# A row sum over 16,384 rows: one row a partition loaded first, and a tail of 15 rows a partition

## The chip, the core and the metric

The kernel runs on one core of one Trainium2 chip. The metric is the time on the device in microseconds (us), the median of several runs. The engines used are VectorE (DVE in the profile), ScalarE (ACT) and SyncE (SP), whose queue issues every DMA. TensorE does nothing here and GpSimd (POOL) only sets four constants. The 16 DMA engines of the core move the data between the chip's memory (HBM) and the on-chip memory, which has 128 partitions.

## The reference

```python
def setup_inputs():
    batch, seq, dim = 32, 512, 1024
    return {
        "x": np.random.randn(batch, seq, dim).astype(np.float32),
        "multiplier": 0.5,
    }

def reference(x, multiplier):
    return (np.sum(x, axis=-1) * multiplier).astype(np.float32)
```

x has 32 x 512 = 16,384 rows of 1024 float32 numbers (4 KB a row, 67.1 MB in all). Each row becomes one number: its sum times 0.5. The output is 64 KB.

## The kernel before

Each of the 128 partitions handles 128 rows. The rows lie in two regions of x. The first region, `x_rows`, gives each partition 112 consecutive rows (`own`), so that neighbouring partitions' rows lie 112 x 4 KB = 448 KB apart. The second, `x_last`, gives each partition 16 consecutive rows, 64 KB apart from partition to partition.

The first region is worked off in seven blocks of 16 rows a partition (line 105). A block is one load of 8.4 MB into one of three buffers `xb`; in it each partition has one stretch of 64 KB. VectorE sums the block in one instruction into `sums` (line 117) and scales the sums into `res` (line 123). A load into a buffer waits until VectorE has summed what lay there (line 77, by the counts in `freed`). In the seventh block VectorE sums eight rows, and ScalarE the other eight, one `activation` with an accumulator each (line 82).

The second region is the tail (lines 137 to 172). It goes into the next buffer in three pieces, rows 0 to 7, 8 to 12, and 13 to 14; row 15 goes into a tile of its own, `end`, in two parts of 608 and 416 columns. Each part has a semaphore. The set `on_act` says which rows ScalarE takes; VectorE takes the others with `dve_sum` (line 92), which adds the halves of a row and accumulates. The two parts of row 15 are summed by VectorE, `first` and `final`, where the second takes up the sum of the first through one column of `end`.

All DMAs stand on SP's queue in program order: seven blocks, three pieces, two parts of the last row, then the store of the first region's results (`early`, line 150, 448 bytes a partition), then the store of the tail's results (line 175, 64 bytes a partition). `early` waits for the seventh block's sums on both engines, the last store for the `final` sum and for ScalarE's last row. At the end SP waits for both stores.

`start_loads_at_entry` (line 182) moves the loads at the head of SP's queue that wait for nothing, up to the first one that waits, from the body of the program to its entry, ahead of the barrier at which all engines meet. These are the first three blocks' loads.

Of the kernel before, what the change touches and what calls it, by code (L numbers as in the profile page):

```python
# [8 lines left out]
@with_exitstack  # L9
def kernel(  # L10
    ctx: ExitStack,
    tc: tile.TileContext,
    x: bass.AP,
    multiplier: float,
    out: bass.AP,
):

    nc = tc.nc
    tc.close()
    tc.compile()  # L26
    nc.switch_body("work")

    P = nc.NUM_PARTITIONS
    fp32 = mybir.dt.float32  # L30
    ADD = mybir.AluOpType.add

    x_flat = x.flatten_outer_dims()
    N, D = x_flat.shape
    rows = N // P
    out_flat = out.rearrange("b s -> (b s)")
    mul = float(multiplier)

    B = 16
    n_blocks = rows // B  # L40
    assert N == P * rows and rows == n_blocks * B
    own = rows - B
    x_rows = x_flat[0 : P * own, :].rearrange("(p c) d -> p c d", p=P)
    x_last = x_flat[P * own : N, :].rearrange("(p c) d -> p c d", p=P)
    out_rows = out_flat[0 : P * own].rearrange("(p c) -> p c", p=P)
    out_last = out_flat[P * own : N].rearrange("(p c) -> p c", p=P)

    def sbuf(name, *shape):
        return ctx.enter_context(nc.sbuf_tensor(name, list(shape), fp32)).ap()

    bufs = 3
    buf = [sbuf(f"xb{i}", P, B, D) for i in range(bufs)]
    sums = sbuf("sums", P, rows)
    res = sbuf("res", P, rows)
    cut = 608
    at = 640
    end = sbuf("end", P, at + D - cut)

    def sem(name):
        return nc.alloc_semaphore(name=name)  # L60

    dve_done = sem("dve_done")
    act_done = sem("act_done")
    counts = {"dve": 0, "act": 0}

    def marks(i, engine):

        s = dve_done if engine == "dve" else act_done
        i.then_inc(s, 1)
        counts[engine] += 1  # L70
        return counts[engine]

    def load(name, dst, src, free=None):
        landed = sem(name)
        i = nc.sync.dma_start(out=dst, in_=src)  # L75
        if free is not None:
            i.wait_op(dve_done, free, "sem-ge")
        i.then_inc(landed, 16)
        return landed

    def act_row(t, r, col):
        return nc.scalar.activation(  # L82
            out=t[:, r, :],
            in_=t[:, r, :],
            func=mybir.ActivationFunctionType.Copy,
            scale=mul,
            accum_out=res[:, col : col + 1],
        )

    def dve_sum(row, dst, scale):  # L90
        mid = row.shape[-1] // 2
        return nc.vector.tensor_tensor_reduce(  # L92
            out=row[:, 0:mid],
            in0=row[:, 0:mid],
            in1=row[:, mid:],
            scale=scale,
            scalar=0.0,
            op0=ADD,
            op1=ADD,
            accum_out=dst,  # L100
        )

    marks(nc.vector.memset(end[:, at - 2 : at], 0.0), "dve")  # L103
    freed = []
    for b in range(n_blocks - 1):
        c0 = b * B
        t = buf[b % bufs]
        landed = load(
            f"landed{b}",
            t,  # L110
            x_rows[:, c0 : c0 + B, :],
            freed[b - bufs] if b >= bufs else None,
        )
        h = B if b < n_blocks - 2 else B // 2
        nc.vector.wait_ge(landed, 16)
        done = marks(
            nc.vector.reduce_sum(  # L117
                out=sums[:, c0 : c0 + h], in_=t[:, 0:h, :], axis=mybir.AxisListType.X
            ),
            "dve",  # L120
        )
        freed.append(done)
        scaled = nc.vector.tensor_single_scalar(  # L123
            out=res[:, c0 : c0 + h],
            in_=sums[:, c0 : c0 + h],
            scalar=mul,
            op=mybir.AluOpType.mult,
        )
        scaled.wait_op(dve_done, done, "sem-ge")
        early_dve = marks(scaled, "dve")  # L130
        if h < B:
            nc.scalar.wait_ge(landed, 16)
            for r in range(h, B):
                i = act_row(t, r, c0 + r)
            early_act = marks(i, "act")

    c0 = (n_blocks - 1) * B
    t = buf[(n_blocks - 1) % bufs]
    nc.sync.wait_ge(dve_done, freed[n_blocks - 1 - bufs])
    pieces = [(0, 8), (8, 13), (13, 15)]  # L140
    landed = [
        load(f"landed_p{k}", t[:, lo:hi, :], x_last[:, lo:hi, :])
        for k, (lo, hi) in enumerate(pieces)
    ]
    landed_end = [
        load(f"landed_e{k}", end[:, to : to + hi - lo], x_last[:, B - 1, lo:hi])
        for k, (to, lo, hi) in enumerate(((0, 0, cut), (at, cut, D)))
    ]
    nc.sync.wait_ge(dve_done, early_dve)
    early = nc.sync.dma_start(out=out_rows, in_=res[:, 0:own])  # L150
    early.wait_op(act_done, early_act, "sem-ge")
    early_stored = sem("early_stored")
    early.then_inc(early_stored, 16)

    on_act = {4, 5, 6, 7, 11, 12, 14}
    for k, (lo, hi) in enumerate(pieces):
        on = [r for r in range(lo, hi) if r in on_act]
        nc.scalar.wait_ge(landed[k], 16)
        for r in on:
            i = act_row(t, r, c0 + r)  # L160
        late_act = marks(i, "act") if k == len(pieces) - 1 else None
        on = [r for r in range(lo, hi) if r not in on_act]
        nc.vector.wait_ge(landed[k], 16)
        for r in on:
            dve_sum(t[:, r, :], res[:, c0 + r : c0 + r + 1], mul)
    nc.vector.wait_ge(landed_end[0], 16)
    first = dve_sum(end[:, 0:cut], end[:, at - 1 : at], 1.0)

    first.then_inc(landed_end[1], 1)
    final = dve_sum(end[:, at - 2 :], res[:, rows - 1 : rows], mul)  # L170
    final.wait_op(landed_end[1], 17, "sem-ge")
    done = marks(final, "dve")

    nc.sync.wait_ge(act_done, late_act)
    store = nc.sync.dma_start(out=out_last, in_=res[:, own:])
    store.wait_op(dve_done, done, "sem-ge")
    stored = sem("stored")
    store.then_inc(stored, 16)
    nc.sync.wait_ge(early_stored, 16)
    nc.sync.wait_ge(stored, 16)  # L180

    def start_loads_at_entry(nc_):

        entry, *rest = nc_.main_func.blocks
        is_sp = lambda i: i.engine == mybir.EngineType.SP
        is_load = lambda i: type(i).__name__ == "InstDMACopy"
        for block in rest:
            body = list(block.instructions)  # L190
            own = [i for i in body if is_sp(i)]
            if not any(is_load(i) for i in own):
                continue
            lead = []
            for i in own:
                if not is_load(i) or i.sync_info.on_wait:
                    break
                lead.append(i)
            names = {i.name for i in lead}
            block.instructions = [i for i in body if i.name not in names]  # L200
            head = list(entry.instructions)
            at = next(
                k for k, i in enumerate(head) if is_sp(i) and type(i).__name__ == "InstDrain"
            )
            entry.instructions = head[:at] + lead + head[at:]
            return

    nc.at_finalize(start_loads_at_entry)
# [35 lines left out]
```

## Time and profile before

| | |
|---|---|
| median of 3 runs | 160.66 us (160.62 to 160.91) |
| span of the profiled execution | 159.43 us |
| HBM read and written | 67.11 MB and 0.07 MB |
| mean over the span | 421 GB/s |
| VectorE, one block of 16 rows (line 117) | 17.22 us, 6 times |
| VectorE, eight rows (line 117) | 8.69 us, once |
| ScalarE, one row and its read (line 82) | 1.04 us from one to the next, 15 times |
| VectorE, one row with `dve_sum` and its read (line 92) | 0.69 and 0.08 us, 8 times |
| from a block load's issue to its landing | 40.8 us (median of 7) |
| early store, from issue to landing | 10.8 us |
| last store, from issue to landing | 1.4 us |

The profile is one execution. Its times count from the start of its first instruction, SP's first DMA issue. In a line of the timeline the first number is the start, the second the duration; then come the engine, the line of the kernel, the operation, what it writes and reads, and in brackets how long the engine had idled before it and what ended that. "DMA xb<-in_x_dram" as the releaser means that a load landed. SPq is SP's DMA queue: its durations are those of the issue and not of the transfer. A load's transfer runs on all 16 DMA engines; each engine works through its own share of the queue, packet by packet. On the page a chain of work is given that is followed back from the last instruction, with the share of the span that each engine has in it.

### The profile page before, as it was taken

How to read it: one execution, taken by the hardware profiler on the slowest of the kernel's cores; microseconds unless marked ns; L12 is line 12 of the kernel's file. 1: busy time of each engine (PE TensorE's matmuls, PEld its weight loads, DVE VectorE, ACT ScalarE, POOL GpSimd, SP SyncE). 2: the span in 40 equal slices, each digit the busy share in tenths (PEclk: the TensorE clock that was granted, in tenths of full speed). 3: DMA queues.
4: the chain of work that ended last, by engine and by line, in shares of the span. 5: the costliest groups of instructions: out<-in, count | busy, mean ns of one | idle time of the engine just before them, and what ended most of it. 6: DMA issues, size and time to landing. Idle time of an engine off the chain costs nothing.

```text
span 159.4 us, 122 instructions
## 1 busy us (share of the span) xinstructions
DVE 119.3 (75%) x35; ACT 17.3 (11%) x31; POOL 0.2 (0%) x4
## 2 busy tenths in 40 slices
DVE  0000059998699978999599995999959999598644
ACT  3000000000000000000000000000000000397954
POOL 0000000000000000000000000000000000000000
DMA  7996996996999979969969969969979799698994
GB/s 263 526 526 263 526 510 280 526 510 280 526 395 395 526 312 477 526 296 493 526 263 526 526 263 526 510 280 526 477 312 526 345 444 526 280 501 364 421 410 145
DMA packets 2016, 67.18 MB, mean 421 GB/s; under 512 B 480, under 2 KB 608, under 8 KB 736
## 3 DMA queue, kind: packets, MB, share of 16 engines
q1 hardware_dynamic: 2016, 67.18, 98.0%
HBM read 67.11 MB, written 0.07 MB: 421 GB/s over the span
## 4 chain that ended last, share of the span: by engine, by line
DMA 76%; DVE 22%; SPq 1%; issue 0%
DMA xb<-in_x_dram 51%; DMA end<-in_x_dram 25%; DVE sums L117 22%; SPq L75 1%; DVE end L92 1%; DVE res L123 0%; DVE res L92 0%
## 5 line engine op out<-in xcount | busy, mean ns | idle before, releaser
L117 DVE TENSOR_REDUCE sums<-xb 128x16 f32<-128x16384 f32 (+1 forms) x7 | 112.0, 16001 | 30.9 <-DMA xb<-in_x_dram 30.9
L82 ACT ACTIVATE xb<-xb 128x1024 f32<-128x1024 f32 x15 | 15.7, 1044 | 137.7 <-DMA xb<-in_x_dram 137.7
L92 DVE CUSTOM_DVE_ANT_0 xb<-xb 128x512 f32<-128x512 f32 x8 | 5.1, 688 | 4.9 <-DMA xb<-in_x_dram 4.9
L82 ACT ACTIVATION_READ_ACCUMULATOR xb<-xb 128x1 f32 x15 | 2.8, 186 | 0.0
L103 DVE MEMSET end<- 128x2 f32 x1 | 0.1, 60 | 2.5 <-PEq L26 2.5
L82 ACT ACT_TABLE_LOAD x1 | 1.3, 1283 | 2.4 <-PEq L26 2.4
L123 DVE TENSOR_SCALAR res<-sums 128x16 f32<-128x16 f32 (+1 forms) x7 | 1.2, 174 | 0.2
L92 DVE CUSTOM_DVE_ANT_0 end<-end 128x304 f32<-128x304 f32 (+1 forms) x2 | 0.9, 426 | 0.1
L92 DVE DVE_READ_ACCUMULATOR2_ANT res<- 128x1 f32 x9 | 0.7, 82 | 0.0
L225 POOL MEMSET const-bfloat16-1.0<- 128x1 bf16 x1 | 0.1, 102 | 0.0
L225 POOL MEMSET const-uint8-127<- 128x1 uint8 x1 | 0.1, 102 | 0.0
L225 POOL MEMSET const-float32-1.0<- 128x1 f32 x1 | 0.1, 99 | 0.0
L225 POOL MEMSET const-float32-0.0<- 128x1 f32 x1 | 0.1, 98 | 0.2 <-issue 0.2
L92 DVE DVE_READ_ACCUMULATOR2_ANT end<- 128x1 f32 x1 | 0.1, 81 | 0.0
## 6 DMA issues: line engine op xcount, KB each, us to landing
xb<-in_x_dram SPq DMA_DIRECT2D x1, 4096.0 KB, 31.2
xb<-in_x_dram SPq DMA_DIRECT2D x1, 2560.0 KB, 36.9
xb<-in_x_dram SPq DMA_DIRECT2D x1, 1024.0 KB, 38.9
end<-in_x_dram SPq DMA_DIRECT2D x1, 304.0 KB, 39.1
end<-in_x_dram SPq DMA_DIRECT2D x1, 208.0 KB, 39.2
xb<-in_x_dram SPq DMA_DIRECT2D x7, 40.8
out_dram<-res SPq DMA_DIRECT2D x1, 56.0 KB, 10.8
out_dram<-res SPq DMA_DIRECT2D x1, 8.0 KB, 1.4
```

What stands on the lines that cost most here:

```text
L75: i = nc.sync.dma_start(out=dst, in_=src)
L82: return nc.scalar.activation(out=t[:, r, :], in_=t[:, r, :], func=mybir.ActivationFunctionType.Copy, scale=mul, accum_out=res[:, col : co ...
L92: return nc.vector.tensor_tensor_reduce(out=row[:, 0:mid], in0=row[:, 0:mid], in1=row[:, mid:], scale=scale, scalar=0.0, op0=ADD, op1=ADD, ...
L103: marks(nc.vector.memset(end[:, at - 2 : at], 0.0), "dve")
L117: nc.vector.reduce_sum(out=sums[:, c0 : c0 + h], in_=t[:, 0:h, :], axis=mybir.AxisListType.X),
L123: scaled = nc.vector.tensor_single_scalar(out=res[:, c0 : c0 + h], in_=sums[:, c0 : c0 + h], scalar=mul, op=mybir.AluOpType.mult,)
L225: nc = _bacc.Bacc("TRN2", target_bir_lowering=False, num_devices=1)
```

## The change

128 consecutive rows, the last ones of x, are taken out of the tail. They are a region of their own, `x_lead`, with one row to a partition, so that neighbouring partitions' rows lie next to each other. They are loaded first of all, into a new tile `lead`, with 4 KB a partition; VectorE sums and scales them in one `dve_sum` ahead of block 0's sum, into a new tile `lead_res`. That load waits for nothing, so it is among those that are moved to the entry, four now. Its result has a store of its own, 4 bytes a partition, on SP's queue right behind the early store, and SP waits for it at the end.

The tail's region has 15 rows a partition: 60 KB from partition to partition in x, 60 bytes a partition in the output. Piece 0 has seven rows instead of eight, the pieces behind it have as many as before, and ScalarE takes three of the first piece's rows instead of four. The other rows are split as before. The last store moves 60 bytes a partition instead of 64.

```diff
@@ -40,10 +40,14 @@
     own = rows - B
+    tail = B - 1
+    lead0 = P * (own + tail)
     x_rows = x_flat[0 : P * own, :].rearrange("(p c) d -> p c d", p=P)
-    x_last = x_flat[P * own : N, :].rearrange("(p c) d -> p c d", p=P)
+    x_last = x_flat[P * own : lead0, :].rearrange("(p c) d -> p c d", p=P)
+    x_lead = x_flat[lead0:N, :].rearrange("(p c) d -> p c d", p=P)
     out_rows = out_flat[0 : P * own].rearrange("(p c) -> p c", p=P)
-    out_last = out_flat[P * own : N].rearrange("(p c) -> p c", p=P)
+    out_last = out_flat[P * own : lead0].rearrange("(p c) -> p c", p=P)
+    out_lead = out_flat[lead0:N].rearrange("(p c) -> p c", p=P)
@@ -55,6 +59,8 @@
+    lead = sbuf("lead", P, 1, D)
+    lead_res = sbuf("lead_res", P, 1)
@@ -102,6 +108,7 @@
     freed = []
+    lead_landed = load("lead_landed", lead, x_lead)
     for b in range(n_blocks - 1):
@@ -112,6 +119,9 @@
         h = B if b < n_blocks - 2 else B // 2
+        if b == 0:
+            nc.vector.wait_ge(lead_landed, 16)
+            marks(dve_sum(lead[:, 0, :], lead_res, mul), "dve")
         nc.vector.wait_ge(landed, 16)
@@ -137,13 +147,13 @@
-    pieces = [(0, 8), (8, 13), (13, 15)]
+    pieces = [(0, 7), (7, 12), (12, 14)]
...
-        load(f"landed_e{k}", end[:, to : to + hi - lo], x_last[:, B - 1, lo:hi])
+        load(f"landed_e{k}", end[:, to : to + hi - lo], x_last[:, tail - 1, lo:hi])
@@ -151,8 +161,11 @@
     early_stored = sem("early_stored")
     early.then_inc(early_stored, 16)
-
-    on_act = {4, 5, 6, 7, 11, 12, 14}
+    lead_store = nc.sync.dma_start(out=out_lead, in_=lead_res)
+    lead_stored = sem("lead_stored")
+    lead_store.then_inc(lead_stored, 16)
+
+    on_act = {4, 5, 6, 10, 11, 13}
@@ -167,16 +180,17 @@
-    final = dve_sum(end[:, at - 2 :], res[:, rows - 1 : rows], mul)
+    final = dve_sum(end[:, at - 2 :], res[:, rows - 2 : rows - 1], mul)
...
-    store = nc.sync.dma_start(out=out_last, in_=res[:, own:])
+    store = nc.sync.dma_start(out=out_last, in_=res[:, own : own + tail])
...
     nc.sync.wait_ge(early_stored, 16)
+    nc.sync.wait_ge(lead_stored, 16)
     nc.sync.wait_ge(stored, 16)
```

## The prediction

> **What bounds the kernel now.** I read the shares of busy time first, then the groups of instructions, then the chain of work that ended last, then the timeline around each landing, and last the windows at both ends. From the page:
>
> ```profile
> span 159.4 us, 122 instructions
> DVE 119.3 (75%) x35; ACT 17.3 (11%) x31; POOL 0.2 (0%) x4
> q1 hardware_dynamic: 2016, 67.18, 98.0%
> DMA 76%; DVE 22%; SPq 1%; issue 0%
> L117 DVE TENSOR_REDUCE sums<-xb 128x16 f32<-128x16384 f32 (+1 forms) x7 | 112.0, 16001 | 30.9 <-DMA xb<-in_x_dram 30.9
> ```
>
> The one load queue holds the 16 DMA engines busy for 98.0% of the span, and all 30.9 us that VectorE idles ahead of its block sums end with a landing. The timeline says why the chain's 22% on VectorE is no limit of its own:
>
> ```profile
> 21.91 17.22 DVE L117 TENSOR_REDUCE sums<-xb 128x16 f32<-128x16384 f32 x1 [19.40 <-DMA xb<-in_x_dram]
> 41.22 17.22 DVE L117 TENSOR_REDUCE sums<-xb 128x16 f32<-128x16384 f32 x1 [1.88 <-DMA xb<-in_x_dram]
> 137.97 8.69 DVE L117 TENSOR_REDUCE sums<-xb 128x8 f32<-128x8192 f32 x1 [1.92 <-DMA xb<-in_x_dram]
> 147.69 0.69 DVE L92 CUSTOM_DVE_ANT_0 xb<-xb 128x512 f32<-128x512 f32 x1 [0.82 <-DMA xb<-in_x_dram]
> 153.78 0.69 DVE L92 CUSTOM_DVE_ANT_0 xb<-xb 128x512 f32<-128x512 f32 x1 [3.55 <-DMA xb<-in_x_dram]
> 156.27 0.69 DVE L92 CUSTOM_DVE_ANT_0 xb<-xb 128x512 f32<-128x512 f32 x1 [0.57 <-DMA xb<-in_x_dram]
> 157.03 0.47 DVE L92 CUSTOM_DVE_ANT_0 end<-end 128x304 f32<-128x304 f32 x1
> 157.56 0.38 DVE L92 CUSTOM_DVE_ANT_0 end<-end 128x209 f32<-128x209 f32 x1
> 157.97 0.34 SPq L175 DMA_DIRECT2D out_dram<-res  x1
> ```
>
> Blocks land every (137.97-41.22)/5 = 19.35 us and take 17.22 + 0.17. A block is 8.389 MB, so the steady rate is 8.389/19.35 = 433.5 GB/s. The bytes of x at that rate are 67.11/0.4335 = 154.8 us. The rest of the span is a head (block 0 lands at 21.91, that is 2.56 us later than its 19.35 of data) and an end of some 1.9 us behind the last landing at 157.54 (0.38 for the final sum, the store issued at 157.97, landed 1.4 later). So three things set the time: bytes over rate, head, end.
>
> The head, in windows that count a packet's bytes where it starts (columns: window, length, VectorE, ScalarE and GpSimd busy, clock, DMA share, GB/s):
>
> ```profile
> 0.00:0.99 0.99, 0.00 (x0) 0.00 (x0) 0.20 (x4) 1.00 0.00 0
> 0.99:1.70 0.71, 0.00 (x0) 0.00 (x0) 0.00 (x0) 1.00 4.09 1385
> 1.70:2.20 0.50, 0.00 (x0) 0.00 (x0) 0.00 (x0) 1.00 0.00 0
> 2.20:2.25 0.05, 0.00 (x0) 0.00 (x0) 0.00 (x0) 1.00 3.02 1311
> 4.00:4.50 0.50, 0.00 (x0) 0.00 (x0) 0.00 (x0) 1.00 4.54 1966
> 4.60:4.65 0.05, 0.00 (x0) 0.00 (x0) 0.00 (x0) 1.00 3.02 1311
> ```
>
> A partition's share of a block is 64 KB, one packet. 1385 x 0.71 / 65.5 KB = 15 packets start in 0.99 to 1.70; one engine starts alone after 2.20. The second packets start at 4.00 to 4.50 (15) and after 4.60 (1). In the steady part 128 packets on 16 engines take 19.35 us, so one takes 2.42 us: the 15 early engines need 0.3 to 0.9 us too long for their first packet, the late one does not, and ends last. By the trace's semaphore arrivals it also ends last in every later load, the final one included.
>
> **The change, part by part.**
>
> *Bytes.* The last region gives up 128 rows (0.524 MB) and the lead load takes the same 128 rows. Moved, not added: 0.
>
> *One more load in the queue.* Its price is what a short load takes beyond its bytes. Piece 2 (1.049 MB) lands 156.27-153.78 = 2.49 us behind piece 1, its bytes need 2.42: +0.07. The first part of the end row (0.311 MB) took 0.74 and needs 0.72: +0.02. The lead load has as many packets as these (one a partition, 4 KB). I take **+0.07** (0.02 to 0.10). The shorter piece 0 saves no packet: 28 KB a partition instead of 32.
>
> A page speaks against this step: the Trainium skill, "DMA: Bandwidth & Descriptors", section "Anatomy of one DMA — SWDGE (gpsimd) path", puts a fixed cost of about 2.0 us on every DMA beside its bytes. By that rule the sum would come out at an estimated 162.7 us; the rows above show 0.02 to 0.07 for a load that follows others in this queue, so the rule does not add up along a queue here.
>
> *The head.* The lead load is issued first (SP, 0.37 us for a first issue), block 0 then starts its issue at some 0.42 instead of 0. Its packets come up 0.42 later, but the lead's 1.21 us of data runs meanwhile, so the queue is not empty: 0 if the slow first packets are a cost of starting that is paid once. The trace has no first load of 4 KB packets; the bounds are the two ends of the row of windows: up to -0.6 (the last engine's second packet at 4.63 against the first one's at 4.01) if short packets start all engines alike, up to +0.9 if block 0 pays the slow first packet again behind the lead. The nearest row is the change of load at every later landing, 19.35 apart with nothing between, so I take **0**.
>
> *SP's entry.* Four issues instead of three stand ahead of SP's drain and the start barrier: +0.42 us for the other engines' first instructions (VectorE's memset at 2.45, ScalarE's table load at 2.38). Their cover is the wait for the first landings (until some 3.8 and 138 us): 0. Without it, 0.42.
>
> *The lead's sum.* One 0.69 us sum and its 0.08 us read on VectorE, with a wait for the lead ahead of block 0's wait. Behind that wait stands only VectorE's queue, which would have slept until 21.9. Lead lands at about 2.56 + 1.21 = 3.8, sum done by 4.6, block 0 at 21.91 + 1.28 = 23.19: hidden by 18 us. Uncovered, 0.77.
>
> *Everything between.* All blocks land 1.21 + 0.07 = 1.28 us later; buffers come free 1.28 later too, and a reload is issued over 20 us ahead of when its data is wanted (block 3 at 39, wanted at 80): 0. The last reduce moves to 139.25 and ends, with its scaling, at 148.14 instead of 146.86. Piece 0 lands at 147.69 + 0.07 = 147.76, now before VectorE is free: this wait turns from DMA to VectorE, and its four sums end at 148.14 + 4 x 0.61 = 150.6. Piece 1 lands at 153.85: 3.2 us of cover. ScalarE is done with its eight rows at 147.7 and with three more by 150.9. From piece 1 on rows, splits and engines are as before. 0.
>
> *Stores.* The early store moves from 146.96 to about 148.24 and the lead store is issued behind it (0.35 us) by 148.95; SP then waits for ScalarE until 157.4 as it does now, so 8.5 us cover both. Their packets stand behind all loads on the rings. At the end:
>
> ```profile
> 156.40:157.30 0.90, 0.83 (x3) 0.90 (x2) 0.00 (x0) 1.00 0.66 226
> 157.30:158.80 1.50, 0.60 (x4) 0.12 (x2) 0.00 (x0) 1.00 0.00 0
> 158.80:159.05 0.25, 0.00 (x0) 0.00 (x0) 0.00 (x0) 1.00 0.37 33
> ```
>
> The early store's packets are through by 157.30, the final store's run from 158.80: 1.5 us in which the queue is empty. The lead store has 8 packets of 4 bytes an engine; the final store moves 128 packets of 64 bytes within 0.25 us, so 4-byte packets at that pace fit six times: 0, as long as one takes under 1.5/8 = 0.19 us. The wait for it stands ahead of the wait for the final store and costs only beyond that.
>
> The final store shrinks from 64 bytes a partition, each on a 64-byte boundary, to 60 bytes at a pitch of 60, on none. No row shows a store off such a boundary. Lower bound -0.02 (a sixteenth of the 0.25 us); upper bound +0.6, if everything from its first packet to its landing (158.8 to 159.4) doubles. 448-byte and 64-byte stores both pass without a stall, so I take **+0.05**.
>
> **Sum.** 0.07 + 0 + 0.05 = +0.12: span 159.43 to 159.55, and with the 1.23 us between span and median (160.66 - 159.43) 160.78 us. A change under 0.2% (0.32 us) is about what a measurement of this kernel can't tell from none; the three runs span 0.29.
>
> **Rivals.**
>
> 1. *The slow first packets are paid twice (slower).* For: nothing in the trace says whether the 0.3 to 0.9 us belongs to starting a queue or to the first touch of the rows of a block, which lie 448 KB apart; the lead's rows lie side by side. Against: later packets go to rows as far apart at full pace. Price: 0.3 to 0.9, middle 0.6, with the 0.12: 161.4 us. It decides once block 0's landing is over 1.28 + 0.3 later, past 23.5. The skill's fixed 2.0 us a DMA named above is the extreme of this rival, and the trace so far gives it a 1 in 50.
>
> 2. *Small stores that share lines (slower).* If a 4-byte write takes over 0.19 us, the final store waits on its rings; if the 60-byte ones stall too, they land late. Price: at 0.3 us a packet the lead store ends at 157.3 + 2.4 = 159.7, which is 0.9 past 158.8, so the end moves by 0.9; the final store's own doubling gives 0.6. Middle 0.6 over the 0.07: 161.3. Against: the cheap 64-byte packets. The Trainium skill, same page, section "Specifications", has transfers under 512 bytes done as read-modify-write; both of today's stores are under that and this trace shows no stall in either, while 4 bytes is untried here.
>
> 3. *A shorter head (faster).* Short first packets bring all engines up together, and the late engine, which ends last to the end, is late no more. Gain 0.18 (level with the next one, 4.63 against 4.45) to 0.6; near the upper part, 0.5, less the 0.12: 160.3 us. For: that engine starts 0.5 us behind all others on 64 KB packets. Against: the start of an engine may not depend on the packets' size.
>
> 4. *No effect at all*, the head costing nothing and the store as before, 160.7, belongs to the forecast: the DMA-bound chain cannot use the earlier start of VectorE.
>
> **How the numbers follow.** Forecast with no. 4: 0.42, own range 160.45 to 161.05, nearly all of it within 0.2%. Rival 1: 0.22, rival 2: 0.16, together slower by more. Rival 3: 0.20, of which a part stays within 0.2%. So faster 0.19, same 0.41, slower 0.40. The range for 8 in 10 takes in rival 3's 160.3 and both slower ones at their middle: 160.2 to 161.5.
>
> **What would show it.** Head: block 0's reduce starts at 23.2 (forecast), past 23.5 (rival 1), under 22.9 (rival 3), and the start of the second packets of the last engine. Middle: landings 19.35 apart, last reduce 1.28 later, four sums that no longer wait for piece 0. End: the last landing at 157.6, and from the final store's issue to its landing 1.4 us (forecast) or more (rival 2), with packets of the lead store in the window that is empty now. I am wrong if the head moves by more than 0.3 us either way, or if the store's 1.4 us does.

## The result, and the profile after

| | before | after |
|---|---|---|
| median | 160.66 us | 164.53 us (164.44 to 164.69) |
| span of the profiled execution | 159.43 us | 163.2 us |
| last store, from issue to landing | 1.4 us | 5.2 us |

The ratio is 1.0236, with a 95% interval of 1.0222 to 1.0250: 3.9 us slower, outside the range of 160.2 to 161.5 and not the "no change" that was forecast.

From the page of the changed kernel:

```profile
span 163.2 us, 125 instructions
q1 hardware_dynamic: 2304, 67.18, 95.8%
DMA 74%; DVE 22%; SPq 1%; issue 0%
```

The queue's share fell from 98.0 to 95.8%: 4.2% of 163.2 us is 6.9 us in which, as a mean over the 16 engines, it moved no packets, against 3.2 us before. So the added time is not spent moving data. The chain view does not show it, because its 23 to 25 pieces end with the last work of an engine and leave out the store behind that. The timeline of the changed kernel shows where the kernel still was on time:

```profile
3.39 0.69 DVE L98 CUSTOM_DVE_ANT_0 lead<-lead 128x512 f32<-128x512 f32 x1 [0.40 <-DMA lead<-in_x_dram]
22.87 17.22 DVE L127 TENSOR_REDUCE sums<-xb 128x16 f32<-128x16384 f32 x1 [18.78 <-DMA xb<-in_x_dram]
42.33 17.22 DVE L127 TENSOR_REDUCE sums<-xb 128x16 f32<-128x16384 f32 x1 [2.03 <-DMA xb<-in_x_dram]
139.08 8.69 DVE L127 TENSOR_REDUCE sums<-xb 128x8 f32<-128x8192 f32 x1 [1.92 <-DMA xb<-in_x_dram]
147.88 0.68 DVE L98 CUSTOM_DVE_ANT_0 xb<-xb 128x512 f32<-128x512 f32 x1
148.45 0.43 SPq L164 DMA_DIRECT2D out_dram<-lead_res  x1
157.45 0.38 DVE L98 CUSTOM_DVE_ANT_0 end<-end 128x209 f32<-128x209 f32 x1
157.86 0.33 SPq L188 DMA_DIRECT2D out_dram<-res  x1
```

The last row's second sum starts at 157.45 and the last store is issued at 157.86, both 0.11 us *earlier* than before (157.56 and 157.97). All the loss lies behind the last instruction that computes. The list of DMA issues (KB each, us from issue to landing) and the waits of SP's queue say on what:

```profile
out_dram<-res SPq DMA_DIRECT2D x1, 56.0 KB, 14.7
out_dram<-lead_res SPq DMA_DIRECT2D x1, 0.5 KB, 14.5
out_dram<-res SPq DMA_DIRECT2D x1, 7.5 KB, 5.2
```

```profile
SPq L187 <- ACT xb L88: 8.5, 1, 8.5
SPq L193 <- DMA out_dram<-lead_res: 4.8, 1, 4.8
```

The lead store, 0.5 KB in 128 writes of 4 bytes, was issued at 148.45 and landed 14.5 us later, at 162.95. SP stands at line 193, which is the wait for it, for 4.8 us. The last store took 5.2 us instead of 1.4. The windows at the end show that no packets ran meanwhile (DMA share and GB/s are the last two columns):

```profile
157.20:158.60 1.40, 0.60 (x4) 0.13 (x2) 0.00 (x0) 1.00 0.00 0
158.60:158.95 0.35, 0.00 (x0) 0.00 (x0) 0.00 (x0) 1.00 0.26 22
158.95:163.20 4.25, 0.00 (x0) 0.00 (x0) 0.00 (x0) 1.00 0.00 0
```

By packets the lead store was through before 157.20 and the last store by 158.95; the records give a 4-byte packet 9 ns. A store is done, however, when all 16 DMA engines have reported that it landed, and those reports trickled in. In order of arrival (us):

```
early store 157.14 157.18 157.19 157.25 157.27 157.28 157.30 157.31 157.36 157.47 157.48 157.56 161.27 161.57 162.26 162.78
lead store  157.35 157.49 157.71 158.11 158.50 158.50 159.55 159.87 160.85 161.17 161.28 161.44 161.75 162.36 162.93 162.95
last store  159.12 159.13 159.16 159.17 159.18 159.25 159.75 160.07 161.03 161.33 161.46 161.62 161.92 162.53 163.10 163.11
```

From the seventh on, each report of the last store comes 0.16 to 0.21 us behind one of the lead store. The six reports ahead of these come at 159.1 to 159.3, much as all 16 did before (159.2 to 159.4). A report does not name its engine, so that these pairs belong to one engine each is inferred from their order and their even distance.

The early store is late too, which is the 14.7 us above instead of 10.8: four of its reports come at 161.3 to 162.8, although its packets stood ahead of the lead store's.

### The profile page after: what moved, and what is told of

It is laid out like the page before. It is cut to its first block, busy times and chain, and to the rows that moved or that the text cites. A ratio compares the mean times of both kernels' runs of the same rounds, so it can differ in the third digit from the quotient of the medians.

```text
span 163.2 us, 125 instructions
## 1 busy us (share of the span) xinstructions
DVE 119.9 (73%) x37; ACT 16.3 (10%) x29; POOL 0.2 (0%) x4
## 3 DMA queue, kind: packets, MB, share of 16 engines
q1 hardware_dynamic: 2304, 67.18, 95.8%
## 4 chain that ended last, share of the span: by engine, by line
DMA 74%; DVE 22%; SPq 1%; issue 0%
DMA xb<-in_x_dram 50%; DMA end<-in_x_dram 23%; DVE sums L127 21%; SPq L81 1%; DVE end L98 1%; DVE res L133 0%; DVE res L98 0%
## 5 line engine op out<-in xcount | busy, mean ns | idle before, releaser
L88 ACT ACTIVATE xb<-xb 128x1024 f32<-128x1024 f32 x14 | 14.6, 1045 | 138.2 <-DMA xb<-in_x_dram 138.1
L98 DVE CUSTOM_DVE_ANT_0 lead<-lead 128x512 f32<-128x512 f32 x1 | 0.7, 692 | 0.4 <-DMA lead<-in_x_dram 0.4
## 6 DMA issues: line engine op xcount, KB each, us to landing
out_dram<-res SPq DMA_DIRECT2D x1, 56.0 KB, 14.7
```

Of the source, the lines that this page charges most:

```text
L88: return nc.scalar.activation(out=t[:, r, :], in_=t[:, r, :], func=mybir.ActivationFunctionType.Copy, scale=mul, accum_out=res[:, col : co ...
L98: return nc.vector.tensor_tensor_reduce(out=row[:, 0:mid], in0=row[:, 0:mid], in1=row[:, mid:], scale=scale, scalar=0.0, op0=ADD, op1=ADD, ...
```

## The experiments

Theory S: the 4-byte writes to neighbouring addresses complete slowly, and the last store is held behind them on the same engines. Rivals: U, the unaligned 60-byte writes of the last store are slow by themselves; E, one more store at the end costs a fixed time, whatever it writes. Ratios are against the kernel before in the same series, whose median was 160.76 to 160.84 us.

### The lead store moved to the start

```diff
+        if b == bufs - 1:
+            lead_store = nc.sync.dma_start(out=out_lead, in_=lead_res)
+            lead_store.wait_op(dve_done, lead_done, "sem-ge")
...
     early.then_inc(early_stored, 16)
-    lead_store = nc.sync.dma_start(out=out_lead, in_=lead_res)
...
```

> The changed kernel with the lead store issued behind the first three loads instead of behind the early store; all else as changed, the 60-byte last store included. Theory S (the 128 writes of 4 bytes to neighbouring addresses complete slowly, and the last store's completion on the same rings stands behind them): the slow writes fall into the middle of the loads, the last store lands 1.4 us after its issue again, 160.6 us. Rival U (the 60-byte writes off every 64-byte boundary are slow by themselves): the last store still lands some 5 us after its issue, 164.5. Rival E (one more store at the end costs a fixed time whatever it writes): 160.6 too; the scratch stores tell it from S.

Measured: 166.21 us, ratio 1.0347 (1.0320 to 1.0375). Half of the expectation came true. The last store, still 60 bytes a partition, lands 1.5 us after its issue, so U falls:

```profile
out_dram<-res SPq DMA_DIRECT2D x1, 7.5 KB, 1.5
```

But the total got worse. Windows over the place where the lead store runs, behind block 2:

```profile
42.20:61.60 19.40, 17.39 (x3) 0.00 (x0) 0.00 (x0) 1.00 1.15 432
61.60:66.50 4.90, 4.90 (x1) 0.00 (x0) 0.00 (x0) 1.00 0.58 94
66.50:86.40 19.90, 12.53 (x3) 0.00 (x0) 0.00 (x0) 1.00 0.95 398
86.40:105.70 19.30, 17.36 (x2) 0.00 (x0) 0.00 (x0) 1.00 1.00 435
```

and in the timeline, block 3:

```profile
61.60 17.22 DVE L132 TENSOR_REDUCE sums<-xb 128x16 f32<-128x16384 f32 x1 [1.97 <-DMA xb<-in_x_dram]
86.37 17.22 DVE L132 TENSOR_REDUCE sums<-xb 128x16 f32<-128x16384 f32 x1 [7.34 <-DMA xb<-in_x_dram]
```

For 4.9 us the starting loads amount to 94 GB/s instead of some 432, and block 3 lands 24.77 us behind block 2 instead of 19.35: +5.4 us, which is the whole difference (166.21 - 160.81). By the packet records of the trace, block 3's first 64 KB packets take 3.3 to 7.3 us on 14 of the 16 engines, and 2.42 us, the usual time, on the other two. The slow writes do not wait aside; they hold up the engines that carry them, and the loads behind. My mistake in the expectation was to take "in the middle of the loads" for cover, where the load queue is what bounds the kernel.

### The kernel before with a scratch store

Six runs add one store to the kernel before, right behind the early store, and change nothing else; the last store has its aligned 64 bytes.

```diff
     early.then_inc(early_stored, 16)
+    scratch = nc.dram_tensor("scratch", (P, 1), fp32, kind="Internal").ap()
+    extra = nc.sync.dma_start(out=scratch[:, 0:1], in_=res[:, 0:1])
+    extra_stored = sem("extra_stored")
+    extra.then_inc(extra_stored, 16)
...
     nc.sync.wait_ge(early_stored, 16)
+    nc.sync.wait_ge(extra_stored, 16)
```

The others have (P, 16) or (P, 4) as the shape, a store from `res[0:16, 0:1]` or `res[0:64, 0:1]`, or the order of places turned, `scratch.rearrange("(b a) o -> a (b o)", a=32)`. The three whose neighbouring partitions do not write side by side also carry the flag `allow_slow_non_contiguous=True`; one of them is slow and two are not, so the flag is not what decides.

> The kernel before with one added store behind the early store: 4 bytes a partition (a column of results) to a scratch tensor in HBM, partitions 4 bytes apart. Theory S: this store takes over 5 us from its packets to its landing and the last store, still 64 bytes a partition, is held behind it: 164.5 (163.5 to 165). Rival U: the last store is aligned, so no change, 160.7. Rival E: 164.5.

Measured: 165.75 us (one run), slow as theory S has it and 0.75 above its range. The lines of the issues:

```profile
scratch<-res SPq DMA_DIRECT2D x1, 0.5 KB, 16.9
out_dram<-res SPq DMA_DIRECT2D x1, 8.0 KB, 6.4
```

> As the run before, but the 128 writes of 4 bytes go 64 bytes apart, so that no two of them fall into one stretch of 64 bytes. If it is the sharing of a stretch that makes them slow (theory S in its narrow form): 160.7. If every write of 4 bytes is slow (S in its wide form) or any added store costs (rival E): 164.5.

Measured: 160.84 us (one run).

```profile
scratch<-res SPq DMA_DIRECT2D x1, 0.5 KB, 10.6
out_dram<-res SPq DMA_DIRECT2D x1, 8.0 KB, 1.4
```

The same 128 writes of 4 bytes by the same instruction cost 5 us side by side and nothing 64 bytes apart. So neither the added store (E), nor the size of 4 bytes alone, nor the number of writes explains it: it is their neighbourhood in HBM. U falls a second time, as the slow run of the two has an aligned last store.

> The kernel before with the added scratch store, its 128 writes of 4 bytes 16 bytes apart: four of them to a stretch of 64 bytes. If writes to one 64-byte stretch go one after another and stretches run side by side (theory L), 5.6 us for 16 of them makes 0.35 each: the store lands 4 x 0.35 = 1.4 us after its packets, within the empty 1.5 us, 160.7 to 161.2. If all 128 go one after another wherever they share a stretch (theory G, 5.6/128 = 44 ns each): 165.5 as at 4 bytes apart.

Measured: 160.84 us (one run). The store lands at 158.69 by the reports, 1.2 us after its packets (1.4 by theory L), inside the cover. Theory G as put here, with 165.5, falls:

```profile
out_dram<-res SPq DMA_DIRECT2D x1, 56.0 KB, 11.4
scratch<-res SPq DMA_DIRECT2D x1, 0.5 KB, 11.2
out_dram<-res SPq DMA_DIRECT2D x1, 8.0 KB, 1.4
```

> The kernel before with a scratch store from 16 partitions alone, 4 bytes each, neighbours: one stretch of 64 bytes in all, one write an engine. Theory L (one after another within a stretch, 0.35 us each): as slow as 128 of them, landing 5 to 6 us after its packets, 165. Theory G (44 ns each over all writes): 0.7 us, 160.8.

Measured: 160.86 us (one run); the store lands at 158.02, 0.7 us after its packets, as the 128 writes 64 bytes apart do (0.6). Theory L falls: sixteen writes into one 64-byte stretch, one an engine, are not slow.

> The kernel before with the scratch store of 128 writes of 4 bytes into the same 512 bytes as at 4 bytes apart, but partition p goes to place (p mod 4) x 32 + p/4: neighbouring partitions, which share a DMA engine, lie 128 bytes apart. Theory G, widened (writes into one stretch of some 512 bytes go one after another, 44 ns each, whoever sends them; it fits 1.1 us at 16 bytes apart and none at 64): 165 to 166 as with neighbours side by side. Theory H (an engine's own successive writes into one small stretch wait for each other, some 0.7 us each): no such neighbours, so 160.9.

Measured: 164.28 us (one run).

```profile
scratch<-res SPq DMA_DIRECT2D x1, 0.5 KB, 15.3
out_dram<-res SPq DMA_DIRECT2D x1, 8.0 KB, 4.9
```

Theory H, as put here, falls: with neighbouring partitions pulled 128 bytes apart, but the same 512 bytes in all, the store is still slow (landed at 162.65). Partitions that are four apart became neighbours, and no trace shows which partitions one engine carries, so a weaker form of H is not excluded. The widened G forecast the slowness, with 0.7 us more of it than came.

> The kernel before with the scratch store of neighbouring 4-byte places from 64 partitions alone, half the writes into half the stretch (256 bytes). Theory G (one write after another, some 40 ns each): 64 x 0.04 = 2.6 us from about 157.3, landing near 160, the last store held until then: span 160.2 to 160.8, time 161.5 to 162. If a stretch that is written by many costs a fixed time whatever the number: as 128 writes, 164 to 166.

Measured: 163.98 us (one run); the store of half as many writes lands at 162.17.

```profile
scratch<-res SPq DMA_DIRECT2D x1, 0.2 KB, 14.8
out_dram<-res SPq DMA_DIRECT2D x1, 8.0 KB, 4.6
```

That misses theory G in its linear form: from their packets to landing 64 writes took 4.7 us, which is 74 ns each, and 128 took 5.3 to 6.9 us (41 to 54 ns each), while 16 took 0.7, about as long as the 128 writes 64 bytes apart. It also lies a hair under the "fixed time" bound. What is shown is that 64 to 128 writes of 4 bytes into one stretch of 256 to 512 bytes complete over some 5 to 7 us. By what law stays open. In every run that has such a store right behind the early store, the early store, whose packets run ahead, also lands late, 14.6 to 17.1 us from its issue, against 10.8 to 11.4 in the other runs with a scratch store.

### The last store on another queue

```diff
-    store = nc.sync.dma_start(out=out_last, in_=res[:, own : own + tail])
+    nc.scalar.wait_ge(act_done, late_act)
+    store = nc.scalar.dma_start(out=out_last, in_=res[:, own : own + tail])
```

> The changed kernel with the last store issued from ScalarE's queue, so that it does not stand on the rings of the lead store; the lead store and the wait for it stay. If only the ring's order holds the last store: it lands some 1.5 us after its issue, while the end still waits for the lead store at 162.9, span 163.0. If the DMA engine itself is held by its slow writes: it lands 5 us after its issue as before, span 163.2. The time is 164.4 to 164.6 in both; the landing tells them apart.

Measured: 165.2 us (one run), span 163.9; that is 0.6 above the range for the time, as the lead store itself took 15.3 us instead of 14.5.

```profile
out_dram<-lead_res SPq DMA_DIRECT2D x1, 0.5 KB, 15.3
out_dram<-res ACTq DMA_DIRECT2D x1, 7.5 KB, 6.0
```

On a queue of its own the last store still takes 6.0 us, and its late reports again follow those of the lead store by about 0.17 us. Five of its reports come at 159.1 to 159.2, and the lead store had five in by then. So what holds it goes engine by engine and not by queue. The Trainium skill, "DMA: Bandwidth & Descriptors", section "Queues, rings and completion order", says of the semaphore's increment that it lands only after every earlier write of that DMA engine, across its queues; this run agrees, with 6.0 us against 1.4. The late reports of the early store are another matter, as the lead store's writes come behind it; why they are late was not tested.

### The change without its store's cost

Two versions keep the lead load and avoid the 128 small writes. In the first, the lead is row 0 of each partition's 16 rows, so its results belong to the last store. The tail has 16 rows again, and all else in it is as in the kernel before:

```diff
-    x_lead = x_flat[lead0:N, :].rearrange("(p c) d -> p c d", p=P)
+    x_lead = x_last[:, 0:1, :]
...
-    pieces = [(0, 7), (7, 12), (12, 14)]
+    pieces = [(1, 8), (8, 13), (13, 15)]
...
-    lead_store = nc.sync.dma_start(out=out_lead, in_=lead_res)
```

> The changed kernel with another lead: row 0 of each partition's 16 rows of the last region, 64 KB apart instead of 4 KB, summed into its column of the results and stored with the others in one last store of 64 bytes a partition; no lead store. Theory S: what the change costs is gone, and what its head gave stays (last landing 0.1 earlier): 160.55, the same as before or 0.1 per cent faster. If the lead load itself costs time: 160.8 or more. Rival U: 160.55 too.

Measured: 161.05 us, ratio 1.0018 (1.0009 to 1.0027). Of the 3.9 us, 0.24 are left. The expected 0.1 us of gain did not come.

The second keeps the rows and gathers the results on the chip:

```diff
+    lead_row = sbuf("lead_row", 1, P)
...
+            gather = nc.sync.dma_start(out=lead_row, in_=lead_res)
+            gather.wait_op(dve_done, lead_done, "sem-ge")
...
-    lead_store = nc.sync.dma_start(out=out_lead, in_=lead_res)
+    lead_store = nc.sync.dma_start(out=out_lead.rearrange("p c -> c p"), in_=lead_row)
+    lead_store.wait_op(gathered, 16, "sem-ge")
```

> The changed kernel with the lead's 128 results first gathered into one partition's row on the chip (128 packets of 4 bytes, issued behind the first three loads, where the early lead store stopped the loads for 5 us) and then stored as one stretch of 512 bytes where the lead store was. If only writes to HBM are slow at 4 bytes: no stop in the loads, last store 1.5 us to landing, and the change without its store's cost remains, 160.6 (160.4 to 160.9; the before of the same runs 160.7). If 4-byte writes into one partition are as slow: 165 or more.

Measured: 161.27 us, ratio 1.0029 (1.0018 to 1.0039), above the expected range. The 128 packets of 4 bytes go into one partition's memory at the very place where the early lead store stopped the loads, and here block 3 follows block 2 after 19.44 us, 0.1 more than usual:

```profile
61.72 17.22 DVE L133 TENSOR_REDUCE sums<-xb 128x16 f32<-128x16384 f32 x1 [2.13 <-DMA xb<-in_x_dram]
81.16 17.22 DVE L133 TENSOR_REDUCE sums<-xb 128x16 f32<-128x16384 f32 x1 [2.01 <-DMA xb<-in_x_dram]
```

So the slowness belongs to HBM as the target. The Trainium skill, "DMA: Bandwidth & Descriptors", section "Why small descriptors are slow (HBM only)", says that transfers within the on-chip memory don't suffer the penalty of small pieces; this run agrees, with 19.44 us against the 24.77 of the store to HBM.

To find the rest, two more:

```diff
-    store = nc.sync.dma_start(out=out_last, in_=res[:, own:])
+    out_60 = out_flat[P * own : N - P].rearrange("(p c) -> p c", p=P)
+    store = nc.sync.dma_start(out=out_60, in_=res[:, own : rows - 1])
```

> The kernel before with a last store of 60 bytes a partition at a pitch of 60 bytes, into the same place of the output, instead of 64 at 64; it leaves the last 128 numbers out and puts the last region's others into the wrong places. If the unaligned 60 bytes cost what the traces with an undisturbed end suggest (1.52 and 1.94 us from issue to landing against 1.41): 160.9 to 161.4, against a before of 160.8. If they cost nothing: 160.8, as before.

Measured: 160.78 us, ratio 1.0004 (0.9995 to 1.0013); issue to landing 1.4 us. 60 bytes at a pitch of 60 cost nothing that can be told.

The last one is the first version with its lead load issued behind block 0's, and its sum taken behind block 0's sum:

```diff
-    lead_landed = load("lead_landed", lead, x_lead)
...
         if b == 0:
+            lead_landed = load("lead_landed", lead, x_lead)
+        if b == 1:
```

> The lead as row 0 of each partition's 16 (no store of its own, a last store of 64 bytes), but loaded second, behind block 0, instead of first. If the 0.2 to 0.3 us that this version cost over the kernel before come from what happens at the head (short packets first, engines out of step): the head is as before and only the queue's price for one more load is left, +0.07, 160.9 with a before of 160.8. If any such load in the queue costs it: 161.1.

Measured: 160.87 us, ratio 1.0010 (1.0001 to 1.0019), +0.10 us: in accord with the queue's price for one load more, 0.07 by the prediction, though the interval reaches from 0.02 to 0.3 us. Loaded first, the same lead cost 0.18%; the intervals overlap, so that the place at the head is what costs the rest is indicated and not shown. The trace of that version has 70 full-size packets after the first 4 us that take over 30 ns too long, against 7 here and 4 in the kernel before. That trace is of one of its slowest runs (161.4 us). In it block 0's sum starts at 23.12, no later than the 23.19 of the prediction, and blocks 3, 5 and 6 come 19.48 to 19.50 us behind the one before instead of 19.35: that run loses its time in the middle of the queue and not at the head. None of the versions beats the kernel before.

## Why the prediction was wrong

**What held.** *Bytes* and *one more load*: +0.10 us measured in the run with the lead loaded second, +0.07 forecast. One row of that estimate was misread: the first part of the end row took 0.76 us by the lines shown (157.03 - 156.27), not 0.74, which makes +0.04 and stays in the range. The section of the Trainium skill that the prediction quotes there for 2.0 us a DMA is on DMAs that GpSimd issues, and SP issues all of these. *SP's entry*: VectorE's and ScalarE's first instructions start 0.48 us later (0.42 forecast) and nothing waits for them. *The lead's sum*: started at 3.39, over by 4.1, 18.8 us ahead of block 0. *Everything between*: the last reduce moved by 1.11 us (1.28 forecast), VectorE goes straight from it to the four sums of piece 0 at 147.88, with no wait for a landing, as told, and the next pieces are met on time. *The last store's 60 bytes*: +0.05 forecast, nothing measured (0.9995 to 1.0013).

**The head** was taken at 0 and is slightly better: block 0's reduce starts at 22.87, 0.32 under the forecast's 23.19. The windows of the changed kernel:

```profile
1.70:2.50 0.80, 0.00 (x0) 0.00 (x0) 0.00 (x0) 1.00 1.03 394
2.50:3.00 0.50, 0.06 (x1) 0.14 (x1) 0.00 (x0) 1.00 4.90 2048
3.00:3.50 0.50, 0.11 (x1) 0.50 (x1) 0.00 (x0) 1.00 0.30 131
```

131 x 0.5 / 65.5 KB is one packet: 15 engines begin block 0 by 3.00 and one after it, 0.17 us behind the 15th by the packet records, instead of 0.5 us behind all others. That is the mechanism of rival 3, at about half of its size, and part of it is gone by the next landing (19.46 us instead of 19.35). The last landing is 0.14 us earlier than before (157.40 against 157.54), where the forecast had it 0.07 later. Rival 1, the slow first packets paid twice, did not happen: block 0's first packets took 2.42 to 2.63 us, where 15 of 16 took 2.7 to 3.3 before.

**What failed** is the step *Stores*, in the sentence that 4-byte packets at the last store's pace fit into the empty 1.5 us six times over, "0, as long as one takes under 1.5/8 = 0.19 us". The packets did keep that pace, at 9 ns each. The step priced a store by how long its packets run, while the end waits for the landing, and no row of the trace before had a store whose writes start less than 64 bytes apart. The lead store landed 5.8 us after its packets, at 162.95, and the last store 0.16 behind it. By itself the last store would have landed 1.4 us after its issue, at 159.27. The difference is 3.8 us, less the 0.1 by which it was issued earlier: 3.7, as the two profiled spans differ (163.2 - 159.4); the medians differ by 3.9. So the term that stood at 0 was worth 3.8 us.

Rival 2 had the right kind of cause, small writes that lie close and a last store that waits on its engines, but priced a write at 0.3 us: eight of them in 5.8 us are 0.7 each, and so it stood at 161.3 instead of 164.5. That writes wait one for another within an engine, as it took them to, is not shown. Its other half, the 60-byte writes, was not there. An unknown with no near row should have had a wide upper bound and not a guess in the middle: eight writes at the 0.6 us that the last store took before from its first packet to its landing are 4.8 us from 157.3, 3.3 past 158.8, which makes 164.0 us and comes near the result.

The Trainium skill's line in "DMA: Bandwidth & Descriptors", section "Specifications", that transfers under 512 bytes are done as read-modify-write, was cited for rival 2. The runs put a limit to it: 448, 64 and 60 bytes, and 4 bytes at 64 apart, are all under it and land without delay; only many small writes into one short stretch were slow (64 or more within 512 bytes).

**Still open:** the law behind the 5 us (64 writes took nearly as long as 128, 16 no longer than usual), why four reports of the early store are late, and the 0.2 to 0.3% of the versions that load the lead first; one trace of them shows the 70 slow packets, the other shows two late reports of the last store (1.9 us to landing), and neither was taken apart further.

## What to carry to other kernels

A store's price is its landing, not its packets: many partitions that each write 4 bytes to neighbouring addresses in HBM took 5 to 7 us to land here, and what the same DMA engines carried behind them, a store of another queue and loads too, was held up. Let small results ride in rows of a store that exists (+0.2% instead of +2.4% here) or gather them on the chip first (+0.3%). Where the load queue bounds the kernel, neither place that was tried hides such a store: moving it from the end to the middle of the loads made it dearer (+3.5% instead of +2.4%). The earlier start of VectorE, which idles anyway, gained nothing.

## What the runs showed of the hardware that was not expected

- 128 writes of 4 bytes: 5.3 to 6.9 us from packets to landing at 4 bytes apart, 1.2 us at 16 apart, 0.6 us at 64 apart; 64 writes at 4 apart took 4.7 us, 16 writes at 4 apart 0.7.
- These writes hold up loads on the same engines: 64 KB packets of 3.3 to 7.3 us instead of 2.42, and a landing 5.4 us late. A store whose packets ran ahead of them reported late too, on four of 16 engines.
- A first load with 4 KB packets lets block 0 land 0.32 us earlier than the sum of its parts, though none of it was left in the measured time of the versions that had no slow store (+0.2 and +0.3%).
